# Memory attention moved to the second half of a two-half encoder layer, and the neighbourhood gates moved to the first

## The chip, the cores and the metric

The kernel runs on one core of one Trainium2 chip. The metric is the time of one execution on the device in microseconds, lower is better; quoted is the median of three runs. A profile is one further execution, recorded instruction by instruction. PE is the matrix engine (TensorE), DVE the vector engine, ACT the scalar engine, POOL the GpSimd engine, and SP the queue from which most DMAs are issued.

## What is computed

One layer of an encoder, for two sequences (4096 and 2048 tokens of 1024 numbers) with shared weights. The reference, cut to what matters:

```python
hn = rms_norm(x, norm_g)
proj = hn @ w_in          # na_q na_k na_v na_g | wq wk wv wg | mq mg
ya = neighbourhood_attention(qa, ka, va, rpb) * silu(na_g)   # 6 heads, 8x16 grid window
yb = windowed_gqa(qb, kb, vb, sink) * silu(wg)               # 6 q heads, 2 kv heads, |t-s| <= 128
yc = memory_attention(qc, km, vm) * silu(mg)                 # 4 heads over 256 memory tokens
y = concatenate([ya, yb, yc]) @ w_out
return x + y
```

Queries and keys are RMS-normed per head of 64; the keys and values of the memory come from a small projection of its own. Every product is made with operands split into a high and a low half of float16 (hi and lo): three matmuls (hi hi, hi lo, lo hi) stand for one product in float32.

## The kernel before

The tokens are cut into 24 groups of 256 (16 and 8 for the two sequences), each of two blocks of 128. The kernel has two halves with a change of buffers between them (the seam).

**First half.** For each block, x is loaded, normed, transposed on PE against an identity (line 527) and kept as hi and lo; a copy goes to DRAM (xTd). The projection (`proj`, lines 302, 303, 305) makes a 512-wide chain "a", a 512-wide "b" and a 384-wide "v" of 24 matmuls each. "a" holds the neighbourhood queries and the queries of two of the four memory heads, "b" those of the other two and the neighbourhood keys. The 16 heads are normed (POOL raises to a power, line 311) and transposed on PE, eight transposes per block (line 729). The neighbourhood attention of a group has six units (three head pairs, two kinds of column blocks): scores (line 903), bias and row minimum on DVE (line 920), exponential on ACT (930), hi and lo of the weights (956, 965), one DMA transpose of 12 blocks of 128x128 (`pt<-phl`, line 971), and the product with the values (986). The memory attention of a group has four units of two heads: scores (1042), row minimum (1058), exponential (1064), hi (1078), lo (1084), one DMA transpose of 8 blocks (`ptm<-phm`, line 1092), the product with the memory values (1104). The results of both are stored to DRAM as float32 (`od<-oev`). Beside this the weights of the second half are scaled, split and stored to DRAM.

**Second half.** For each block two 320-wide chains "tok" make the windowed queries, keys and values. For each group eight gate chains of 24 matmuls of 256 columns (lines 1270 to 1272), tanh on ACT (1277) and one DVE step (1282) make `sg`. Windowed attention (1321, 1332 to 1355, DMA transposes of 6 blocks, 1373) follows. The stored results of the other two groups of heads are loaded (`ot<-od`), multiplied by the gates (1413), split to hi and lo (1397, 1403) and go through the output projection (1448 to 1450) with the residual.

The order on every engine is written at build time by a planner (`Plan.run`): tasks with a priority, an assumed duration, buffer counts and dependences are played through, and each engine's instructions are emitted in the order in which the play starts them. On the chip each engine's queue is in order. PSUM has eight banks: two `pj` for projections and gates, four `sc` for scores and transposes, two `po` for attention results. All DMA transposes are issued from SP.

At the seam `f_T2`, `f_TC` and `f_T3` close the pools of the first half and open those of the second; `f_Wa` and `f_Wb` put the second half's weights where the first half's stood, as soon as the last projection has read them. The second group's x (`x2`) lies in a pool that opens at `f_TC`, after the last memory product:

```python
t_x = pl.add("sp", 0.2, f_x, (x_use if gs_ == 0 else [t_TC, t_x]) + [x_st[2 * gs_], x_st[2 * gs_ + 1]], ...)
```

Of the kernel before, what the change touches and what calls it, by code (L numbers as in the profile page):

```python
# [8 lines left out]
F16 = mybir.dt.float16  # L9
# [24 lines left out]
WIN_ORDER = tuple(range(0, 384)) + tuple(range(2560, 2816)) + tuple(range(384, 1152)) + tuple(  # L34
    1536 + 64 * (j + 3 * v) + d for j in range(3) for v in range(2) for d in range(64)) + tuple(range(1920, 2176)) + tuple(
    range(1152, 1536)) + tuple(
# [158 lines left out]
def build(tc, A, out, seqs):  # L195
# [35 lines left out]
    o_d = [[drp.tile([P, 256], F32, name=f"od{g}_{c}", tag=f"od{g}_{c}") for c in range(5)] for g in range(NSB)]  # L231
    mkv_d = [drp.tile([P, 2048], F16, name=f"mkvd{s}", tag=f"mkvd{s}") for s in range(len(seqs))]
    W2 = {"t": 640, "g": D, "o": D}
# [16 lines left out]
    aA, aE = ct("aA", [P, 16]), ct("aE", [P, 16])  # L250
    wA, wE = ct("wA", [P, 8]), ct("wE", [P, 8])
    mA, mE = ct("mA", [P, 4]), ct("mE", [P, 4])
    hg, oc, btmp = ct("hg", [P, 1]), ct("oc", [P, 1]), ct("btmp", [P, 8])
    SC = {}
    for nm in "abvmtgo":
# [8 lines left out]
    for k, n in {"x": 2, "sq": 1, "xhl": 1, "rawm": 2, "sqm": 2, "mkhl": 2, "xT": 2, "raw": 2, "qhl": 1, "khl": 1, "qT": 3, "vhl": 2,  # L264
                 "va": 4, "pf": NPF, "phl": NPHL, "pt": 4, "oev": 3, "pfm": 2, "phm": 2, "ptm": 2, "bE": 2,
                 "ring": 4, "qn": 2, "mkv": 1,
                 "x2": 2, "xr": 2, "qT2": 3, "vw": 8, "pf2": 4,
                 "phl2": 3, "pt2": 2, "tg": 2, "sg": 9, "ot": 4, "yT": 10, "ring2": NR2}.items():
        pl.cap(k, n)
# [116 lines left out]
    wa = pools["WS"].tile([P, 2, NK, 1024], F16, tag="wa", name="wa", bufs=1)  # L386
    wb = pools["WS"].tile([P, 2, NK, 384], F16, tag="wb", name="wb", bufs=1)
    one("SU", "w1f", [P, NK, 1408], F32)
# [3 lines left out]
    W1 = {"a": wa[:, :, :, 0:512], "b": wa[:, :, :, 512:1024], "v": wb, "m": wm}  # L392
# [7 lines left out]
    for s in range(len(seqs)):  # L400
        if s > 0:
            mkv_views(s, one("SM", f"mkvs{s}", [P, 2048], F16))
        for b in range(2):
            one("SM", f"xm{s}{b}", [P, 16, P], F16)
# [36 lines left out]
    for nm, c0, n, src, fl, pr, parts in (("a", 0, 512, w_in, "w1", -29.09, 4), ("b", 512, 512, w_in, "w1", -27.0, 2),  # L441
                                          ("v", 1024, 384, w_in, "w1", -23.0, 2), ("m", 0, 512, A["w_mem_kv"], "wm", -20.0, 2)):
# [3 lines left out]
        for pt_ in range(parts):  # L446
            ks = slice(nk_ * pt_, nk_ * pt_ + nk_)

            def f_l(ks=ks, c0=c0, n=n, src=src, fl=fl):
# [3 lines left out]
                       slack={"v": 12.77, "m": 38.18, "b": 5.95}.get(nm, 0.0))  # L453
# [9 lines left out]
            if nm in 'abvm':  # L463
# [3 lines left out]
        t = scale_tasks(nm, g2, g, ts + [tg2_], pr - 30, parts=parts if nm in 'abvm' else 0)  # L467
# [5 lines left out]
        tb = {"a": ((aA, aE, 0, 6, ph[:, 0:1]), (aA, aE, 6, 2, ph[:, 2:3])), "b": ((aA, aE, 8, 2, ph[:, 2:3]), (aA, aE, 10, 6, iph[:, 0:1])),  # L473
              "m": ((mA, mE, 0, 4, iph[:, 2:3]),)}.get(nm, ())
# [6 lines left out]
    w1_use = [t for nm in "abv" for t in t_w[nm]]  # L481
    su_use = list(t_w["m"])

    def f_TA():
# [4 lines left out]
        mkv_views(0, tile_of("YA", ("mkv", 0), "mkv", [P, 2048], F16))  # L489
    t_TA = pl.add("free", 0.0, f_TA, w1_use, acq=["mkv"], label="TA")  # L490
# [3 lines left out]
    def x_tasks(src, dst_alloc, pr, deps=(), tag=None, acq=()):  # L494
# [25 lines left out]
        for hf in range(2):  # L520
# [9 lines left out]
            t = pl.add("pe", 0.45, f_T, [t, t_id], prio=px - 1.0, acq=[bk] + (list(acq) if hf == 0 else []), rel=["x"] if hf else [], label="xT")  # L530
            if hf:
                x_use.append(t)

# [11 lines left out]

    for i in range(2 * len(seqs)):
# [14 lines left out]
        t_e = pl.add("act", 0.8, f_e, [t_p, t_TA], prio=-3, acq=["rawm"], label="mev")  # L561
# [28 lines left out]
        elif s == 0:  # L590
            t_mk = t_mk0 + [t_kT, t_v]
            su_use += t_mk
        else:
            def f_ms(s=s):
                SY.dma_start(out=mkv_d[s], in_=st[f"mkvs{s}"])
            t_ms = pl.add("sp", 0.1, f_ms, t_mk0 + [t_kT, t_v], prio=-3, label="mst", xf=1.8)
            su_use.append(t_ms)
# [20 lines left out]
    for bt, nm, kw, nr in (("bA", "A", 32, 11), ("bB", "B", 24, 12)):  # L618
        def f_b(bt=bt, nm=nm, n=nr * kw):
            SY.dma_start(out=st[bt], in_=A["rpb" + nm][:, :, 0:n])  # L620
            mk = tile_of("YM", ("mk", nm), "pfm", [P, 2, 256], F32).rearrange("p a k -> p (a k)")[:, 0:n]
            st["mk", nm] = mk
            SY.dma_start(out=mk, in_=A["c_m" + nm])
        t = pl.add("sp", 0.2, f_b, [t_T1], prio=0.9, acq=["pfm"], label="bias", xf=3.0)
# [4 lines left out]
        t_bias.append(pl.add("pool", 4.93, f_b2, [t], prio=0.9, rel=["pfm"], label="bias2"))  # L629
# [5 lines left out]
    kT_done, q_done, qm_done, v_done, xa_use = {}, {}, {}, {}, []  # L635
    x_st = {}
    prev_qk = []
    for gs_ in range(NSB):
        s, g, n = sbs[gs_]
        for blk in range(2):  # L640
# [3 lines left out]
            t_xT = x_tasks(xin[s][row:row + P, :], lambda nb=nb: tile_of("XA", ("xT", nb), "xT", [P, 16, P], F16), pr,  # L644
                           tag=nb, acq=["xT"])
            t_xst = pl.add("pool", 1.04, lambda nb=nb: G.dma_start(out=xT_d[nb], in_=st["xT", nb]), [t_xT], prio=pr + 0.2,
# [3 lines left out]
            def mk_pg(key, n, k0=0, k1=NK, nb=nb):  # L650
                def f():
                    proj(bank("pj", key, nb)[:, 0:n], st["xT", nb], W1[key][:, 0], W1[key][:, 1], slice(0, n), k0, k1)
                return f

            def mk_ev(key, o, n, nb=nb):
                def f():
                    if o == 0:
                        tile_of("X0", ("raw", nb), "raw", [P, 16, HD], F32)
# [7 lines left out]
            for key, nn, o in (("a", 512, 0), ("b", 512, 512)):  # L666
# [12 lines left out]
            pl.add("free", 0.0, lambda: None, [t_p["v"], t_xst], rel=["xT"], label="f")  # L679
            wa_last, wb_last = [t_p["a"], t_p["b"]], [t_p["v"]]  # L680
# [17 lines left out]
            def f_red(nb=nb):  # L698
                st["r16", nb] = small("X0", "r16", 3, 16)
                V.tensor_reduce(out=st["r16", nb], in_=st["sq", nb].rearrange("p (h d) -> p h d", d=HD), axis=AX.X, op=ALU.add)  # L700
            t_red = pl.add("dve", 1.14, f_red, [t_e["b"]], prio=pr - 0.2, rel=["sq"], label="red")
            t_r = pl.add("pool", 3.5, lambda nb=nb: rnorm(st["r16", nb], aA, aE, 16), [t_red] + t_tab,
                         prio=pr - 0.2, label="r16")

            def f_nrm(nb=nb):
                raw = st["raw", nb]
                V.tensor_tensor(out=raw, in0=raw, in1=st["r16", nb].unsqueeze(2).to_broadcast([P, 16, HD]), op=ALU.mult)
            t_nrm = pl.add("dve", 1.14, f_nrm, [t_r], prio=pr - 0.2, label="nrm")

            def f_kg(nb=nb):  # L710
                k = st["raw", nb][:, 10:16]
# [7 lines left out]
            def f_T(i, nb=nb, bks=bks, gs_=gs_, blk=blk):  # L719
                if i == 0:  # L720
                    if blk == 0:
                        tile_of("YA", ("qT", gs_), "qT", [P, 3, 2, 4, 64], F16)
                    tile_of("YA", ("qn", nb), "qn", [P, 2, 2, P], F16)
                raw = st["raw", nb]
                for c in range(4):
                    o = bank(*bks[i])[:, P * c:P * c + P]
                    if i == 0 and c < 3:
                        o = o.rearrange("p (b r c) -> p r b c", r=2, b=4)
                    T.transpose(o, raw[:, 8 * i + 2 * c:8 * i + 2 * c + 2].rearrange("p h d -> p (h d)"), ident)
            t_qk0 = pl.add("pe", 0.5, lambda f_T=f_T: f_T(0), [t_nrm, t_TA, t_id] + prev_qk[0:1], prio=pr - 1.2,  # L730
                          acq=[bks[0], "qn"] + (["qT"] if blk == 0 else []), label="qT")
# [826 lines left out]
```

## Time and profile before

| | |
|---|---|
| median of 3 runs | 2733.17 us (2722.15 to 2733.46) |
| profiled execution | 2732.95 us, of which span 2731.1 us |
| mean granted clock of PE | 0.978 of full speed |
| busy: PE, DVE, ACT, POOL | 2590.1, 1879.7, 1272.5, 543.4 us |
| PE without work, 137 to 1161 us | 82.7 us |
| PE without work, 1161 to 1300 us | 25.4 us |
| PE without work, 1300 to 2732 us | 5.5 us |

The span is the time from the first to the last instruction. A matmul's recorded duration overlaps with the next one's, so the pace of PE is read from start to start and not from durations; idle time of PE is time with no matmul in flight.

### The profile page before, as it was taken

How to read it: one execution, taken by the hardware profiler on the slowest of the kernel's cores; microseconds unless marked ns; L12 is line 12 of the kernel's file. 1: busy time of each engine (PE TensorE's matmuls, PEld its weight loads, DVE VectorE, ACT ScalarE, POOL GpSimd, SP SyncE). 2: the span in 40 equal slices, each digit the busy share in tenths (PEclk: the TensorE clock that was granted, in tenths of full speed). 3: DMA queues.
4: the chain of work that ended last, by engine and by line, in shares of the span. 5: the costliest groups of instructions: out<-in, count | busy, mean ns of one | idle time of the engine just before them, and what ended most of it. 6: DMA issues, size and time to landing. Idle time of an engine off the chain costs nothing.

```text
span 2731.1 us, 58589 instructions
## 1 busy us (share of the span) xinstructions
PE 2590.1 (95%) x22150; PEld 1600.3 (59%) x22150; DVE 1879.7 (69%) x5370; ACT 1272.5 (47%) x3685; POOL 543.4 (20%) x738
## 2 busy tenths in 40 slices
PE   5989888999998899978999999999999999999999
PEld 3545454555554555556666666666666666666665
DVE  6477777888777778885865665666666656566664
ACT  7456555666666667673433333333333333333332
POOL 2553233333322543321000000000000000000000
PEclk9999999999999999988999999999999999999999
DMA  5488997989998998899645444454454435455443
GB/s 182 141 160 175 190 194 186 188 191 201 206 198 181 212 212 168 169 211 261 143 101 105 100 107 106 110 122 112 111 113 104 104 90 106 106 112 122 109 95 76
DMA packets 707467, 401.38 MB, mean 147 GB/s; under 512 B 617648, under 2 KB 654160, under 8 KB 706544
## 3 DMA queue, kind: packets, MB, share of 16 engines
q1 hardware_dynamic: 691312, 347.10, 60.7%
q0 software_dynamic: 15872, 50.55, 5.4%
q8 instruction: 173, 2.83, 0.4%
q14 instruction: 110, 0.90, 0.1%
HBM read 160.54 MB, written 87.03 MB: 91 GB/s over the span
## 4 chain that ended last, share of the span: by engine, by line
PE 56%; DMA 1%; DVE 1%; issue 0%; ACT 0%; POOL 0%; SPq 0%; DVEq 0%; ACTq 0%; POOLq 0%
PE bank L1270 7%; PE bank L1448 6%; PE bank L1271 6%; PE bank L1272 6%; PE bank L1449 6%; PE bank L1450 6%; PE bank L302 4%; PE bank L303 4%; PE bank L305 4%; PE bank L1321 3%; PE bank L1373 3%; DMA pt<-phl 1%; DVE phl L965 0%; PE bank L986 0%; DVE pf L920 0%
## 5 line engine op out<-in xcount | busy, mean ns | idle before, releaser
L1270 PE MATMUL bank<-x,wb 128*128 128x256 f16 x1152 | 315.2, 274 | 0.0
L1271 PE MATMUL bank<-x,wb 128*128 128x256 f16 x1152 | 314.0, 273 | 0.0
L1272 PE MATMUL bank<-x,wa 128*128 128x256 f16 x1152 | 314.0, 273 | 0.0
L1338 ACT ACTIVATE pf<-pf,sm 128x384 f32<-128x384 f32 (+1 forms) x288 | 172.6, 599 | 300.6 <-DVE sm L1332 299.5
L302 PE MATMUL bank<-wa,xT 128*128 128x512 f16 x768 | 299.3, 390 | 4.4 <-DVE vhl L689 3.8
L303 PE MATMUL bank<-wa,xT 128*128 128x512 f16 x768 | 297.9, 388 | 0.7 <-DVE wa L364 0.6
L1448 PE MATMUL bank<-wo,yT 128*128 128x512 f16 x768 | 291.3, 379 | 0.0
L1449 PE MATMUL bank<-wo,yT 128*128 128x512 f16 x768 | 291.1, 379 | 0.0
L1450 PE MATMUL bank<-wo,yT 128*128 128x512 f16 x768 | 291.1, 379 | 0.0
L309 POOL TENSOR_TENSOR r<-r,wA 128x8 f32<-128x8 f32 x48 | 10.3, 215 | 1276.3 <-DVE r L1223 1276.3
L1277 ACT ACTIVATE tg<-bank,hg 128x256 f32<-128x256 f32 x192 | 89.6, 467 | 364.0 <-PE bank L1272 364.0
L311 POOL TENSOR_TENSOR r<-r,mhalf 128x16 f32<-128x16 f32 (+2 forms) x100 | 223.8, 2238 | 7.8
L930 ACT ACTIVATE pf<-pf,sm 128x288 f32<-128x288 f32 (+3 forms) x288 | 156.1, 543 | 128.0 <-DVE sm L920 125.9
L302 PE MATMUL bank<-wa,x 128*128 128x320 f16 x768 | 213.3, 301 | 1.0 <-DMA x<-xTd 1.0
L303 PE MATMUL bank<-wa,x 128*128 128x320 f16 x768 | 213.0, 301 | 0.0
L1463 DVE SCALAR_TENSOR_TENSOR xr<-bank,oc,xr 128x512 f32<-128x512 f32 x96 | 71.9, 749 | 197.8 <-PE bank L1450 197.8
L1332 DVE CUSTOM_DVE_ANT_0 pf<-bank,wtab,nsink 128x384 f32<-128x384 f32 (+1 forms) x288 | 163.9, 599 | 58.6 <-PE bank L1321 58.5
L302 PEld LDWEIGHTS <-xT 128*128 128x128 f16 x1152 | 115.2, 100 | 124.8 <-issue 25.1
L303 PEld LDWEIGHTS <-xT 128*128 128x128 f16 x1152 | 115.1, 100 | 114.5 <-issue 16.3
L305 PE MATMUL bank<-wa,xT 128*128 128x512 f16 x768 | 181.4, 379 | 0.0
L305 PEld LDWEIGHTS <-xT 128*128 128x128 f16 x1152 | 112.8, 98 | 115.7 <-issue 0.3
L1355 DVE SCALAR_TENSOR_TENSOR phl<-pf,sm,phl 128x384 f16<-128x384 f32 (+1 forms) x288 | 174.3, 605 | 8.5
(261 smaller groups left out, 5746.1 us busy)
## 6 DMA issues: line engine op xcount, KB each, us to landing
xTd<-xT POOLq DMA_DIRECT2D x48, 512.0 KB, 4.7
x<-xTd SPq DMA_DIRECT2D x48, 512.0 KB
out<-xr SPq DMA_DIRECT2D x48, 512.0 KB
xx<-in_x_prompt SPq DMA_DIRECT2D x32, 512.0 KB
xr<-in_x_prompt SPq DMA_DIRECT2D x32, 512.0 KB
od<-oev POOLq DMA_DIRECT2D x120, 128.0 KB, 3.8
ot<-od SPq DMA_DIRECT2D x120, 128.0 KB
vd<-vhl POOLq DMA_DIRECT2D x48, 192.0 KB, 4.4
```

The source lines that it names most:

```text
L302: T.matmul(ps, xt[:, kk], wh[:, kk, cols], start=(kk == 0), stop=False)
L303: T.matmul(ps, xt[:, kk], wl[:, kk, cols], start=False, stop=False)
L305: T.matmul(ps, xt[:, NK + kk], wh[:, kk, cols], start=False, stop=(kk == NK - 1))
L311: G.tensor_tensor(out=r, in0=r, in1=mhalf[:, 0:n], op=ALU.pow)
L1270: T.matmul(pv, wh, x[:, :, kk, :], start=(kk == 0), stop=False)
L1271: T.matmul(pv, wh, x[:, :, NK + kk, :], start=False, stop=False)
L1272: T.matmul(pv, wl, x[:, :, kk, :], start=False, stop=(kk == NK - 1))
L1338: S.activation(out=pf[:, 0:nk], in_=pf[:, 0:nk], func=AF.Exp, scale=-1.0, bias=sm[:, 0:1], accum_out=sm[:, 1:2])
L1355: V.scalar_tensor_tensor(out=phl[:, nk:2 * nk], in0=st["pfw", u][:, 0:nk], scalar=st["smw", u][:, 3:4], in1=phl[:, 0:nk], op0=ALU.mult, op ...
L1448: T.matmul(ps, yT[:, 0, ts_], st["wo0"][:, c, cs], start=(ci == 0), stop=False)
L1449: T.matmul(ps, yT[:, 0, ts_], st["wo1"][:, c, cs], start=False, stop=False)
L1450: T.matmul(ps, yT[:, 1, ts_], st["wo0"][:, c, cs], start=False, stop=(ci == 7))
```

## The change

Memory attention (scores, softmax, transposes, product) is taken out of the first half and done per group in the second, where its result goes from PSUM straight into the gate product. Its queries are now made by "tok" (448 wide instead of 320) and transposed by the second half's DMA transpose (10 blocks instead of 6) instead of on PE. The first half's "a" and "b" shrink to 384 columns, and the eight PE transposes of a block become six. The three gate chains of the neighbourhood group are computed in the first half from x of both blocks, so x of a group is kept until then. The neighbourhood result is multiplied by its gate there, split, and stored as hi and lo, so that the second half loads it in the form the output projection reads. The memory's keys and values of both sequences go through DRAM. The first half's weights are now one tile `w1` (4 x 384 columns), freed as a whole; the x of the second group, `x2b`, lies in the same tile. The planner's priority shifts are unchanged.

```diff
-    for nm, c0, n, ... in (("a", 0, 512, ...), ("b", 512, 512, ...), ("v", 1024, 384, ...), ("m", ...)):
+    for nm, c0, n, ... in (("a", 0, 384, ...), ("b", 384, 384, ...), ("v", 768, 384, ...), ("n", 1152, 384, ...), ("m", ...)):
...
-                for c in range(4):
+                for c in range(3):
...
+        for c in range(3):
+            def f_g(gs_=gs_, c=c):
+                x, o = st["xT", gs_], slice(128 * c, 128 * c + 128)
+                pv = bank("pj", "n", gs_, c)[:, 0:256].rearrange("p (b t) -> p b t", b=2)
+                for kk in range(NK):
+                    wh, wl = W1["n"][:, 0, kk, o], W1["n"][:, 1, kk, o]
+                    T.matmul(pv, wh, x[:, :, kk, :], start=(kk == 0), stop=False)
+                    T.matmul(pv, wh, x[:, :, NK + kk, :], start=False, stop=False)
+                    T.matmul(pv, wl, x[:, :, kk, :], start=False, stop=(kk == NK - 1))
...
+                V.scalar_tensor_tensor(out=ov, in0=ov, scalar=GSC, in1=st["sgn", gs_, hp], op0=ALU.mult, op1=ALU.mult)
+                S.activation(out=tile_of("YA", ("yhl", gs_, hp), "yhl", [P, 2, 256], F16)[:, 0], in_=st["oev", gs_, hp], func=AF.Copy)
+                V.tensor_tensor(out=yh[:, 1], in0=st["oev", gs_, hp], in1=yh[:, 0], op=ALU.subtract)
...
-    t_Wa = pl.add("free", 0.0, f_Wa, wa_last + prep_done, label="Wa")
-    t_Wb = pl.add("free", 0.0, f_Wb, wb_last + prep_done, label="Wb")
+        w = pools["WS"].tile([P, 24576], F16, tag="w", name="w2", bufs=1)
+        for k, o, n, m in (("wt0", 0, NK, 896), ("wt1", 7168, NK, 896), ("wgb", 18432, 9, 640)):
+        st["x2b"] = w[:, 14336:18432].rearrange("p (b k t) -> p b k t", b=2, k=16)
+    t_W = pl.add("free", 0.0, f_W, w_last + prep_done, label="W")
...
-        t_x = pl.add("sp", 0.2, f_x, (x_use if gs_ == 0 else [t_TC, t_x]) + ...
+        t_x = pl.add("sp", 0.2, f_x, (x_use if gs_ == 0 else [t_W, t_x]) + ...
...
-                    proj(bank("pj", "t", nb, hf)[:, 0:320], ..., slice(320 * hf, 320 * hf + 320))
+                    proj(bank("pj", "t", nb, hf)[:, 0:448], ..., slice(448 * hf, 448 * hf + 448))
...
-                SY.dma_start_transpose(out=tile_of("XB", ("qT", nb), "qT2", [P, 6, P], F16),
+                SY.dma_start_transpose(out=tile_of("XB", ("qT", nb), "qT2", [P, 10, P], F16),
...
-        for c in range(8):          # gates of the second half
+        for c in range(3, 8):
...
+    for gs_ in range(NSB):          # memory attention, now after the windowed attention's tasks
+        prm = Q0 + gs_ + 0.9
+            t_mk = pl.add("sp", 0.1, f_mk, [t_T2, mkv_st[s]], prio=Q0 + gs_ - 0.6, xf=1.82, acq=["mkv"], label="mk")
...           (units as before; buffers pf2 and phl2 shared with the windowed attention)
+                V.scalar_tensor_tensor(out=sg, in0=bank("po", "m", gs_, hp)[:, 0:256], scalar=GSC, in1=sg, op0=ALU.mult, op1=ALU.mult)
...
-        for ci, c in enumerate((0, 1, 2, 6, 7)):
-            ... load ot, multiply by sg, split to hi and lo
+        for c in range(3):
+            def f_o(gs_=gs_, c=c):
+                SY.dma_start(out=tile_of("YB", ("yT", gs_, c), "yT", [P, 2, 256], F16).rearrange("p a t -> p (a t)"), in_=y_d[gs_][c])
+        for c in (6, 7):
+            y_split(c, [y_mem[gs_, c - 6]])
```

## Rows read from the trace of the kernel before

**Rows 1.** Windows: stretch, length, busy PE, PEld, DVE, ACT, POOL, PEclk, DMA, GB/s.
```profile
0.00:137.00 137.00, 108.70 (x550) 57.29 (x551) 76.23 (x187) 77.88 (x149) 53.34 (x76) 0.96 0.48 161
137.00:1161.00 1024.00, 941.35 (x9680) 541.67 (x9680) 807.25 (x2199) 643.30 (x1782) 370.85 (x489) 0.97 0.90 189
478.00:820.00 342.00, 322.90 (x3554) 189.16 (x3553) 275.73 (x737) 231.09 (x624) 114.53 (x154) 0.99 0.95 197
1024.00:1161.00 137.00, 134.68 (x1514) 77.86 (x1514) 111.70 (x317) 92.06 (x265) 46.46 (x60) 1.00 0.85 168
1161.00:1300.00 139.00, 113.59 (x1394) 82.83 (x1389) 97.38 (x324) 76.76 (x246) 28.36 (x42) 0.84 1.03 232
1300.00:2732.00 1432.00, 1426.49 (x10540) 918.52 (x10538) 898.81 (x2662) 474.52 (x1509) 90.86 (x132) 1.00 0.48 107
```

**Rows 2.** Waits of PE, 137 to 1161 us: total us, times, longest.
```profile
PE bank L986 <- DMA pt<-phl: 37.6, 26, 6.6
PE bank L1104 <- DMA ptm<-phm: 20.4, 9, 4.6
PE bank L903 <- DVE sm L920: 5.4, 2, 4.1
...
PE bank L903 <- ACT pfm L1064: 3.4, 1, 3.4
```

**Rows 3.** Waits of PE, 1161 to 1300 us.
```profile
PE bank L986 <- DMA pt<-phl: 19.0, 13, 3.8
```

**Rows 4.** Timeline of SP's queue in the seam: start us, us, line, DMA.
```profile
1161.04 2.54 SPq L1166 DMA_DIRECT2D wa<-w2dt  x4
...
1243.08 1.07 SPq L1186 DMA_DIRECT2D x<-xTd  x2
```

**Rows 5.** Chain that ended last: start us, us, piece of PE work, instructions.
```profile
1123.52 1.30 PE bank L305 x8
...
1129.97 1.73 PE bank L305 x8
...
1139.42 0.76 PE bank L1042 x12
...
1140.83 1.02 PE bank L729 x8
...
1154.01 0.78 PE bank L1104 x12
...
1259.34 1.09 PE bank L305 x8
```

**Rows 6.** Timeline of PE, first and last of a gate's 24 matmuls.
```profile
1415.13 0.28 PE L1270 MATMUL bank<-x,wb 128*128 128x256 f16 x1
...
1417.65 0.27 PE L1272 MATMUL bank<-x,wgc 128*128 128x256 f16 x1
```

**Rows 7.** DMA queues (packets, MB, share of 16 engines) and transposes issued.
```profile
q1 hardware_dynamic: 691312, 347.10, 60.7%
q0 software_dynamic: 15872, 50.55, 5.4%
...
pt<-phl SPq DMA_TRANSPOSE x432
...
ptm<-phm SPq DMA_TRANSPOSE x96
```

**Rows 8.** DVE's groups of instructions, by shape: count, busy us, mean ns, idle before.
```profile
L1084 DVE SCALAR_TENSOR_TENSOR phm<-pfm,smm,phm 128x256 f16<-128x256 f32 x192 | 87.0, 494 | 0.0
L1282 DVE SCALAR_TENSOR_TENSOR sg<-tg,bank 128x256 f32<-128x256 f32 x192 | 79.5, 414 | 122.4 <-ACT tg L1277 122.4
...
L1058 DVE TENSOR_REDUCE smm<-bank 128x2 f32<-128x512 f32 x96 | 63.7, 682 | 14.2 <-PE bank L1042 14.1
...
L1078 DVE TENSOR_SCALAR phm<-pfm,smm 128x256 f16<-128x256 f32 x192 | 61.3, 361 | 6.3 <-DMA ptm<-phm 3.4 <-DVE smm L1071 0.3
...
L1413 DVE SCALAR_TENSOR_TENSOR sg<-ot,sg 128x256 f32<-128x256 f32 x120 | 50.7, 424 | 3.1
```

More of the change, by code (lines that the diff above doesn't have):

```diff
@@ L480, in build @@
                 t_tab.append(t_t)
[L481 removed]
+    w1_use = [t for nm in "abvn" for t in t_w[nm]]
     su_use = list(t_w["m"])
@@ L643, in build, with xT_alloc @@
             pr = gs_ + 0.5 * blk
-            t_xT = x_tasks(xin[s][row:row + P, :], lambda nb=nb: tile_of("XA", ("xT", nb), "xT", [P, 16, P], F16), pr,
-                           tag=nb, acq=["xT"])
-            t_xst = pl.add("pool", 1.04, lambda nb=nb: G.dma_start(out=xT_d[nb], in_=st["xT", nb]), [t_xT], prio=pr + 0.2,
+            def xT_alloc(gs_=gs_, blk=blk):
+                if blk == 0:
+                    tile_of("XA", ("xT", gs_), "xT", [P, 2, 16, P], F16)
+                return st["xT", gs_][:, blk]
+            t_xT = x_tasks(xin[s][row:row + P, :], xT_alloc, pr, tag=nb, acq=["xT"] if blk == 0 else [],
+                           after=x_first[nb - 1] if blk else None)
+            t_xst = pl.add("pool", 1.04, lambda nb=nb: G.dma_start(out=xT_d[nb], in_=st["xT", nb // 2][:, nb % 2]), [t_xT], prio=pr + 0.2,
                            label="xst", slack=1.595, xf=1.46)
@@ L698, in f_red @@
             def f_red(nb=nb):
[L699 to L702, printed above, removed]
+                st["r16", nb] = small("X0", "r16", 3, 12)
+                V.tensor_reduce(out=st["r16", nb], in_=st["sq", nb][:, 0:768].rearrange("p (h d) -> p h d", d=HD), axis=AX.X, op=ALU.add)
+            t_red = pl.add("dve", 0.87, f_red, [t_e["b"]], prio=pr - 0.2, rel=["sq"], label="red")
+            t_r = pl.add("pool", 3.5, lambda nb=nb: rnorm(st["r16", nb], aA, aE, 12), [t_red] + t_tab,
                          prio=pr - 0.2, label="r16")
@@ new lines, in f_T @@
+                raw = st["raw", nb]
+                for c in range(3):
+                    o = bank(*bks[i])[:, P * c:P * c + P]
+                    if i == 0:
+                        o = o.rearrange("p (b r c) -> p r b c", r=2, b=4)
+                    T.transpose(o, raw[:, 6 * i + 2 * c:6 * i + 2 * c + 2].rearrange("p h d -> p (h d)"), ident)
+            t_qk0 = pl.add("pe", 0.38, lambda f_T=f_T: f_T(0), [t_nrm, t_TA, t_id] + prev_qk[0:1], prio=pr - 1.2,
+                           acq=[bks[0]] + (["qT"] if blk == 0 else []), label="qT")
@@ new lines, in build, with views @@
+            t_qk1 = pl.add("pe", 0.38, lambda f_T=f_T: f_T(1), [t_kg, t_qk0] + prev_qk[1:2], prio=pr - 1.2,
+                           acq=[bks[1]] + (["ring"] if blk == 0 else []), rel=["raw"], label="qT")
+            prev_qk = [t_qk0, t_qk1]
+            def views(i, bks=bks, gs_=gs_, blk=blk):
+                bk = bank(*bks[i])[:, 0:384]
+                if i == 0:
+                    return (bk.rearrange("p (h b t) -> p h b t", h=3, b=4),) + tuple(
+                        st["qT", gs_][:, :, v, :, 32 * blk:32 * blk + 32] for v in range(2))
@@ L1379, in build @@
+    for nb in range(NB):
         pl.add("free", 0.0, lambda: None, win_qk[nb], rel=["qT2"], label="f")
-    for nb in range(NB):
         s = sbs[nb // 2][0]
         users = [k for k in (nb - 1, nb, nb + 1) if 0 <= k < NB and sbs[k // 2][0] == s]
-        pl.add("free", 0.0, lambda: None, [t for k in users for t in win_qk[k]], rel=["ring2"], label="f")
+        pl.add("free", 0.0, lambda: None, [t for k in users for t in win_qk[k][0:3]], rel=["ring2"], label="f")
         pl.add("free", 0.0, lambda: None, [win_pv[k] for k in users], rel=["vw"], label="f")
```

445 lines of the change are left out of this document (217 added, 228 removed).

## Prediction

> **What bounds the kernel now.** I read the windows by stage first [rows 1]. From 1300 us to the end PE is without work for 1432 - 1426.5 = 5.5 us only, at full granted clock: the second half is bound by the matrix engine, with DVE busy 899/1432 = 0.63 and the DMA engines 0.48. From 137 to 1161 us PE idles 1024 - 941.4 = 82.7 us, and its clock is granted at 0.97. Of the two levels, 1.2 and 2.4 GHz, that is 6% of the time at the lower one; with PE busy 0.92 of it some 0.03 x 1024 x 0.92 = 28 us are lost to the clock as well. There DVE is busy 0.79 and DMA 0.90. The seam, 1161 to 1300 us, idles 25.4 us at a clock of 0.84, which costs 0.16 x 139 x 0.82 = 18 us more. The start, to 137 us, idles 28.3 us while weights arrive.
>
> Next I asked for whom PE waits in the first half [rows 2]: 58.0 of the 82.7 us are for DMA transposes, 37.6 for those of the neighbourhood weights (`pt`) and 20.4 for those of the memory weights (`ptm`). The rest are single late DVE or ACT steps, one of them a memory exponential (3.4). In the seam 19.0 us are again for `pt` [rows 3].
>
> So the kernel has a half that lacks nothing but PE time and a half that loses 82.7 + 28 = 111 us of 1024, 10.8%, with PE, DVE and DMA all near their limits. The change moves softmax and transposes out of the tight half and matmuls into it.
>
> **The pace of PE.** From the chain of waits [rows 5], per matmul: 512 columns 1.73/8 = 0.2163 us, 384 columns 1.30/8 = 0.1625, 320 columns 1.09/8 = 0.1363. A gate's matmul of 256 columns takes (1417.65 - 1415.13)/23 = 0.1096 us [rows 6]. The trace has no 448-column chain; it lies between the 384 and the 512, and since the three widths lie on a line I take the middle, 0.1894.
>
> **PE's work, by parts.** (1) First-half projections: 24 x (2 x 0.2163 + 0.1625) = 14.28 us per block become 24 x 3 x 0.1625 = 11.70, so -2.58 x 48 blocks = -123.8. (2) "tok": 48 matmuls per block, each 0.1894 - 0.1363 longer, +2.55 x 48 = +122.4 in the second half (+60 to +184 by the 384 and 512 ends, but (1) and (2) are the same columns and should cancel). (3) Gates: 24 groups x 3 chains x 24 x 0.1096 = 189.4 us go from the second half to the first. (4) Memory scores and products: 48 x 0.76 + 48 x 0.78 = 73.9 us [rows 5] go the other way. (5) Two of a block's eight PE transposes are gone: 1.02/8 x 2 x 48 = -12.2; the second half does them by DMA. First half: -123.8 - 73.9 - 12.2 + 189.4 = -20.5. Second half: +122.4 + 73.9 - 189.4 = +6.9. Together **-13.6 us**. This is the sure part, and small; the rest hangs on idle time.
>
> **What leaves the first half on the other engines.** DVE loses the memory units: 87.0 + 63.7 + 61.3 = 212 us [rows 8], and gains, 72 times, one gate step (0.414), one product (0.424) and one split, priced like the product, so 72 x 1.26 = 91. Its share falls from 0.79 to about (807 - 121)/1024 = 0.67, lower still with 12 heads instead of 16 to norm. SP's queue loses 96 transposes. What those cost the DMA engines: POOL's plain DMAs move 50.55 MB in 5.4% of 2731 us, 343 GB/s [rows 7]. By the code the 528 transposes of rows 7 and the 96 of second-half queries and keys are some 4,576 blocks of 32 KB, 150 MB. At 343 GB/s the other 197 MB of SP's queue take 575 us of its 60.7% x 2731 = 1658; 1083 us are left for the blocks, 0.237 us each, 139 GB/s. The 96 x 8 = 768 memory blocks that go are thus 182 us of DMA time, and the share falls from 0.90 to about 0.72.
>
> The Trainium skill (Advanced Engine Details and Errata, X-Bar Transpose (TRN2)) states that transposing DMAs are as fast as regular ones. By that, an estimate from the plain rate above, the move would relieve the DMA engines by 73 us only; the trace disagrees, with 139 against 343 GB/s. The time that such a small relief gives is the first rival below.
>
> **Idle time of the first half.** The nearest row is 1024 to 1161 us, where the second half's weights are already prepared: DVE 0.82, DMA 0.85, clock 1.00, idle 2.3 of 137 us, 1.7%. The first half after the change has less load than that on both, so I take its rate, 1.7% x 1024 = 17 us, and 6 for the change of sequence, where the edge tables are loaded: 23 instead of 82.7, **-60 us**. The clock fell in the windows that idled and not in this one; I leave 8 of its 28 us: **-20 us**. Bounds: nothing gained, if the waits for `pt` only shift, and all 111.
> The gates make PE fuller, but their input is on chip and they wait for no transpose; each needs a `pj` bank for one ACT and one DVE step after 24 x 0.1096 = 2.6 us of matmuls, and two banks cover that. The neighbourhood result's new steps end in a store that nothing reads before the second half: cost nothing, hidden by the whole seam; without that cover the one visible thing is `f_T3`, which waits for the last store.
>
> **The seam.** Now the x of the second group is issued only at 1243 us [rows 4], since its buffer waits for the last memory product. After the change it lies beside the weights and can come 80 us earlier; tok chains of two groups (2 x 96 x 0.1894 = 36 us) and the first group's five gates (13 us) can fill waits for the last `pt`. No memory unit is left to finish there. Against that, all weights share one tile, so no load starts before the last first-half gate, 8 us after the last projection, and the tok weights are 3.67 MB instead of 2.62. Of 25.4 + 18 = 43 us I take **-20**, bounds +16 (the 3.67 MB at the seam's 232 GB/s, uncovered) and -43.
>
> **The second half's waits.** It gets 212 - 91 = 121 us of DVE work or somewhat more (0.71 instead of 0.63), and 768 + 192 blocks, 227 us of DMA (0.64 instead of 0.48). Lower bound: nothing, as now. Upper: the first half's 10.8%, 155 us. The row nearest in load, 1024 to 1161 us, is busier on both and loses 1.7%, which would be 24 us; I take a third, **+8**. Queued behind a late memory product on PE are tok, gate and output chains for the next group, so each wait is paid in full.
>
> **Start and tail.** At the start the first weights come sooner (384 columns of 512), the fourth set later: 0, between -3 and +10 (1.57 MB at 161 GB/s). At the end the last group's memory units stand in DVE's way: 4 x (0.682 + 2 x 0.361 + 2 x 0.494) = 9.6 us at most; I take **+3**.
>
> **Sum.** The profiled execution took 2732.95 us, the median of the runs 2733.17, so it may stand for them. 2732.95 - 13.6 - 60 - 20 - 20 + 8 + 3 = **2630 us**. Its own range, 2585 to 2680: all idle of the first half gone and the seam clean at the low end, half of the gains at the high end.
>
> **Rivals.**
> - *The transposes that go buy little.* The `pt` waits are the transposes' own latency and the planner's order, not crowding. Then 37.6 us of `pt` waits stay and 6 at the change of sequence, 44 instead of 23; clock loss 14 instead of 8; the seam gives 14 instead of 20: 2630 + 21 + 6 + 6 = 2663. For it: at 478 to 820 us DMA is at 0.95 and PE still idles only 19 of 342. Against it: at 0.85 the waits all but vanish.
> - *The seam gets longer.* PE runs dry between the last gate and the first tok, 16 us and 5 of low clock: 2630 + 20 + 21 = 2671. For it: the single tile. Against: two neighbourhood groups are still to be finished then.
> - *Slower: the second half takes over the first half's trouble.* Place: memory transposes of 8 blocks enter SP's in-order queue among the windowed ones, over three shared `phl2` buffers and four `sc` banks, and PE's in-order queue waits for `ptm` or the windowed `pt` as the first half does now. At 10.8%: 2630 - 8 + 155 = 2777. It decides from (2733 - 2630 + 8)/1432 = 7.8% on. For it: the shifts were not set for this order, and 10.8% was lost at DVE 0.79. Against: DVE 0.71, DMA 0.64, and five gates and four tok chains per group that wait for nothing.
> - *No change:* the same at 7 to 8.7%, about 2733.
>
> **Chances.** Forecast 0.55, little relief 0.13, longer seam 0.09, no change 0.08, slower 0.15. A measurement of this kernel tells about 0.5% (14 us) from nothing. The first three are faster by more: 0.77. Range: from 2575, which takes in the upper bounds of the gains, to 2720, past the two weaker gains; outside are the slower case and a sliver.
>
> **What the next profile would show.** Right: PE idle under 40 us between 137 us and the end of the first half, clock 0.99 there, no wait for `ptm` in it, `pt` waits under 20; the first half shorter by about 100 us, the second longer by 10 to 20; DMA share about 0.7 and 0.64, DVE about 0.67 and 0.71. Wrong if PE shows waits for `ptm` or the windowed `pt` in the second half that add up to more than 30 us, if its clock falls there, or if `pt` waits of the first half stay near 38.

## The result, and the profile after

The changed kernel takes 2686.99 us, the median of four runs (2681.55 to 2698.51), against 2731.03 us (2722.15 to 2733.46) for the kernel before, timed beside it: a ratio of 0.985, 95% interval 0.9807 to 0.9894. It is faster, by 44 us, where 103 were forecast. The profiled execution took 2681.55 us (span 2679.4, mean granted clock 0.990), the quickest of the four; two of the others were at a clock of 0.985. Against the profiled execution before (span 2731.1) 51.7 us are to be explained.

The windows by stage, cut as in [rows 1] (the first half ends when the first tok weights are issued, now at 1133 us):

```profile
0.00:137.00 137.00, 109.81 (x661) 69.95 (x662) 73.68 (x185) 80.33 (x157) 54.62 (x83) 0.96 0.52 176
137.00:1133.00 996.00, 936.82 (x10549) 643.27 (x10547) 672.01 (x1772) 590.14 (x1489) 326.78 (x449) 0.99 0.68 167
478.00:820.00 342.00, 327.21 (x3858) 227.91 (x3857) 225.08 (x608) 212.43 (x533) 110.20 (x150) 1.00 0.65 152
1133.00:1300.00 167.00, 148.81 (x1239) 85.13 (x1239) 118.32 (x364) 77.79 (x244) 29.70 (x35) 0.94 0.81 196
1300.00:2680.00 1380.00, 1373.68 (x9611) 772.36 (x9609) 1015.52 (x2964) 516.42 (x1666) 116.19 (x123) 1.00 0.58 124
```

DVE's share of the first half fell from 0.79 to 672/996 = 0.67 and that of the DMA engines from 0.90 to 0.68, about as forecast. PE's idle time there did not follow: 59.2 us where 82.7 were, and 23 were forecast. From 478 to 820 us the DMA share fell from 0.95 to 0.65, and PE idles 14.8 us instead of 19. The second half is as dense as before (6.3 us idle, clock 1.00) although DVE rose to 0.74 and the DMA engines to 0.58.

Waits of PE from 137 to 1133 us: total us, times, longest (compare [rows 2]):

```profile
PE bank L1013 <- DMA pt<-phl: 38.9, 22, 5.7
PE bank L730 <- DVE sm L947: 4.7, 4, 2.3
PE bank L527 <- DVE xx L517: 4.6, 1, 4.6
```

The waits for `ptm`, 20.4 us, are gone with the memory units. Those for `pt`, 37.6 before, are all still there, which the prediction named as a sign that it is wrong. From 1133 to 1300 us (compare [rows 3]), and the second half:

```profile
PE bank L930 <- DVE sm L947: 5.4, 8, 1.6
PE bank L303 <- DMA w<-w2dt: 3.8, 1, 3.8
PE bank L1013 <- DMA pt<-phl: 3.2, 2, 2.4
...
PE bank L302 <- DMA w<-w2dt: 0.8, 1, 0.8
...
PE bank L1342 <- DVE sm L1273: 1.2, 2, 1.0
```

Here the `pt` waits fell from 19.0 to 3.2 us; 4.6 us are a wait for the tok weights. After 1300 us nothing waits for a transpose; L1342, the memory scores, waits 1.2 us for a bank.

SP's queue in the seam (compare [rows 4]), and two pieces of the chain that ended last, a 384-wide and a 448-wide one (compare [rows 5]):

```profile
1131.97 0.92 SPq L1127 DMA_DIRECT2D w<-xTd  x2
1132.94 2.43 SPq L1108 DMA_DIRECT2D w<-w2dt  x4
```

```profile
1119.48 1.30 PE bank L305 x8
...
1182.65 1.51 PE bank L305 x8
```

The second group's x (`w<-xTd`) is now issued at 1132 us instead of 1243, and the weights at 1132.9, after the last gate. The 384-wide matmul takes 1.30/8 = 0.1625 us, as before, and the 448-wide 1.51/8 = 0.1888; 0.1894 was assumed.

DMA queues, and three of the moved or added DVE groups (compare [rows 7, 8]):

```profile
q1 hardware_dynamic: 710176, 346.57, 57.5%
q0 software_dynamic: 13568, 44.25, 4.5%
```

```profile
L1385 DVE SCALAR_TENSOR_TENSOR phl<-pf,smm,phl 128x256 f16<-128x256 f32 x192 | 83.9, 479 | 0.0
L1378 DVE TENSOR_SCALAR phl<-pf,smm 128x256 f16<-128x256 f32 x192 | 59.1, 350 | 25.9 <-DMA pt<-phl 23.5
L1034 DVE SCALAR_TENSOR_TENSOR oev<-oev,sgn 128x256 f32<-128x256 f32 x72 | 32.9, 456 | 2.5
```

The memory softmax costs DVE nearly the same in its new place (479 and 350 ns, 494 and 361 before), and the gate product 456 ns where 424 were assumed.

**Where the 51.7 us came from.** Idle time of PE: first half 82.7 - 59.2 = 23.5, seam 25.4 - 18.2 = 7.2, start 1.1, second half -1.2: 30.6 us. PE's busy time fell by 2590.1 - 2569.1 = 21.0 us. Summed over windows of 10 us, the busy time lost to the lower clock fell from 42.7 to 18.6 us (first half 24.6 to 8.8, seam 14.5 to 6.0), 24 us. So by this estimate all of the fall in busy time is clock, and PE's work itself grew by about 3 us where 13.6 less were forecast.

### The profile page after: what moved, and what is told of

Same layout as the page of the kernel before. It is cut to its first block, busy times and chain, and to the rows that moved or that the text cites. A ratio compares the mean times of both kernels' runs of the same rounds, so it can differ in the third digit from the quotient of the medians.

```text
span 2679.4 us, 57715 instructions
## 1 busy us (share of the span) xinstructions
PE 2569.1 (96%) x22056; PEld 1570.7 (59%) x22056; DVE 1879.5 (70%) x5283; ACT 1264.7 (47%) x3553; POOL 527.3 (20%) x690
## 4 chain that ended last, share of the span: by engine, by line
PE 55%; DMA 4%; DVE 3%; ACT 1%; POOL 0%; issue 0%; SPq 0%; ACTq 0%; DVEq 0%; POOLq 0%
PE bank L1485 6%; PE bank L302 6%; PE bank L1487 6%; PE bank L1486 6%; PE bank L303 6%; PE bank L305 5%; PE bank L1211 4%; PE bank L1213 4%; PE bank L1212 4%; PE bank L1262 3%; PE bank L1314 2%; DMA pt<-phl 1%; PE bank L1405 1%; PE bank L1342 1%; DMA xx<-in_w_out 1%; DVE phl L1296 1%
## 5 line engine op out<-in xcount | busy, mean ns | idle before, releaser
L302 PE MATMUL bank<-w,xT 128*128 128x384 f16 x1152 | 382.8, 333 | 2.3 <-ACT sq L666 1.3
L303 PE MATMUL bank<-w,xT 128*128 128x384 f16 x1152 | 381.4, 332 | 1.0 <-DVE w L364 0.7
L309 POOL TENSOR_TENSOR r<-r,wA 128x12 f32<-128x12 f32 x48 | 16.3, 340 | 1253.2 <-DVE r L1164 1253.2
L311 POOL TENSOR_TENSOR r<-r,mhalf 128x12 f32<-128x12 f32 (+1 forms) x100 | 224.4, 2244 | 7.8
L305 PE MATMUL bank<-w,xT 128*128 128x384 f16 x1152 | 210.9, 326 | 0.0
L992 DVE SCALAR_TENSOR_TENSOR phl<-pf,sm,phl 128x288 f16<-128x288 f32 (+3 forms) x288 | 148.1, 546 | 44.5 <-ACT phl L983 43.4
L983 ACT ACTIVATE phl<-pf,sm 128x288 f16<-128x288 f32 (+3 forms) x288 | 144.8, 545 | 42.0 <-ACT pf L957 22.4
L1291 DVE TENSOR_SCALAR phl<-pf,sm 128x384 f16<-128x384 f32 (+1 forms) x288 | 119.2, 414 | 57.0 <-DMA pt<-phl 40.2
L770 PE MATMUL bank<-xT,w 128*128 128x256 f16 x576 | 157.6, 274 | 0.0
L771 PE MATMUL bank<-xT,w 128*128 128x256 f16 x576 | 157.0, 273 | 0.0
L772 PE MATMUL bank<-xT,w 128*128 128x256 f16 x576 | 157.0, 273 | 0.0
L1364 ACT ACTIVATE pf<-bank,smm 128x256 f32<-128x256 f32 x192 | 88.9, 471 | 123.9 <-DVE smm L1358 122.4
```

The costliest lines, as they stand in the source:

```text
L302: T.matmul(ps, xt[:, kk], wh[:, kk, cols], start=(kk == 0), stop=False)
L303: T.matmul(ps, xt[:, kk], wl[:, kk, cols], start=False, stop=False)
L305: T.matmul(ps, xt[:, NK + kk], wh[:, kk, cols], start=False, stop=(kk == NK - 1))
L311: G.tensor_tensor(out=r, in0=r, in1=mhalf[:, 0:n], op=ALU.pow)
L770: T.matmul(pv, wh, x[:, :, kk, :], start=(kk == 0), stop=False)
L771: T.matmul(pv, wh, x[:, :, NK + kk, :], start=False, stop=False)
```

## The experiments

Ratios are to the kernel before, timed beside each. "First half" is the stretch from 137 us to the issue of the first tok weights, cut anew in each kernel.

### Memory attention left out of either kernel

The memory units (scores, softmax, transposes, products) are left out; the kernel before loads stored neighbourhood results in place of the memory's, the changed one scales the gate alone.

```diff
-    for gs_ in range(NSB):          # before: memory units of the first half
...
+                SY.dma_start(out=tile_of("YB", ("ot", gs_, c), "ot", [P, 256], F32), in_=o_d[gs_][ci % 3])
```
```diff
-    # after: memory units of the second half
...
+                V.scalar_tensor_tensor(out=sg, in0=sg, scalar=GSC, in1=sg, op0=ALU.mult, op1=ALU.mult)
```

> The kernel before, with the memory attention left out of the first half (no scores, softmax, transposes, product or stores of it; the second half loads neighbourhood results in its place, so its work is unchanged). Load theory (the prediction's: waits of the first half come from the load that the memory units put on DVE, the DMA engines and SP's queue): PE loses 74 to 84 us of work, and idle between 137 us and the end of the projections falls from 82.7 to about 25, pt waits from 37.6 to under 15: about 2580 us. Rival, preparation theory (the pt waits come from the preparation of the second half's weights beside it): only the ptm waits and a few late ACT steps go, pt waits stay above 30: about 2620 us.

> The changed kernel, with the memory attention left out of the second half (the gate product reads the gate alone; queries are still made, normed and transposed). If memory costs the second half only its matmuls (48 x 1.54 us and some 100 breaks between chains of 0.09 us): 80 us less, about 2607. If it also makes PE wait or breaks up the order: more than 95 less, below 2592.

Measured: 2626.59 us (0.9625, 0.9608 to 0.9642) for the kernel before without them, 2599.40 us (0.9541) for the changed one. Windows and `pt` waits of the first half of the kernel before without memory:

```profile
137.00:1083.00 946.00, 881.24 (x8888) 499.05 (x8886) 626.94 (x1632) 558.92 (x1429) 349.56 (x448) 0.97 0.75 176
```
```profile
PE bank L986 <- DMA pt<-phl: 39.9, 23, 5.7
```

With DMA at 0.75 and DVE at 0.66 the `pt` waits are 39.9 us; they were 37.6 at 0.90 and 0.79. So relieving DMA and DVE does not shorten them: the load theory behind the -60 us falls, the time is near the 2620 us of the other expectation, and my rival "the transposes that go buy little" names the right mechanism. The traces say the same of the transposes themselves. From the start of its issue on SP to its last completion mark in the trace, a `pt` transpose of the first half took 5.02 us in the mean in the kernel before (124 transposes), 5.04 without memory (130) and 4.91 in the changed kernel (132), at DMA shares of 0.90, 0.75 and 0.68. Leaving out memory attention gave about 103 us in the kernel before and 87.6 in the changed one.

### The neighbourhood gates left out of either kernel

The three chains, their tanh and their DVE step are left out; the neighbourhood result is multiplied by itself in place of its gate.

```diff
-        for c in range(8):
+        for c in range(3, 8):        # before
...
-        for c in range(3): ...       # after: f_g, f_t, f_sg of the first half
```

> The kernel before, with the three neighbourhood gates left out of the second half (their result is squared instead of gated). The second half is paced by PE, so 72 chains of 2.63 to 2.72 us go: 189 to 196 us less, about 2540. If another engine sets the pace of the second half once these are gone: less is gained, above 2560.

> The changed kernel, with the three neighbourhood gates left out of the first half (the result is squared instead of gated; their weights are still loaded and split). If the gates cost their PE time (72 x 2.68 = 193 us) and cover no waits: about 2494. If they fill waits that come back without them (the reason to have them in the half that waits): PE idle of the first half rises by 30 us or more from 54, and the time is above 2520.

Measured: 2541.06 us (0.9313) and 2610.93 us (0.9565). The gates cost about 188 us in the second half, which is their 189 us of matmuls, and only 76 us in the first. The first half of the changed kernel without them, and its longest waits:

```profile
137.00:1085.00 948.00, 797.73 (x9085) 508.27 (x9084) 661.68 (x1774) 566.92 (x1465) 325.00 (x451) 0.91 0.81 177
```
```profile
PE bank L990 <- DMA pt<-phl: 78.0, 26, 7.8
PE bank L730 <- DVE sm L924: 33.0, 9, 10.4
PE bank L907 <- DVE sm L924: 15.7, 9, 6.4
```

PE idles 150 us there, and the clock falls to 0.91: the gates fill time in which PE would wait. Read crosswise, the four kernels say roughly which half of the change pays; roughly, because the memory queries and the new seam go along in both comparisons. With no memory attention anywhere, moving the gates takes 2626.6 to 2599.4, 27 us less. With no gates anywhere, moving memory takes 2541.1 to 2610.9, 70 us more: of the 210 us of PE work that leave the first half (projections, memory, transposes) it gives up 74 (it ends at 1085 us instead of 1159), and most of the rest turns into waits (150 us of idle time instead of 81) and low clock (0.91 instead of 0.96), while the time from there to the end grows from 1382 to 1525 us. Together the two moves give 44 us, because the gates fill what memory leaves. A kernel in which memory alone moves and all gates stay in the second half was not run.

### The preparation of the second half's weights left out

Loads, maxima, scaling and splits are left out and the scales set to one; the stores to DRAM stay, so that the second half reads the same amount.

```diff
-            t = pl.add("sp", 0.1, f_l, ..., label="wpl", ...)     # load, maximum, scale
-                t = pl.add("act", n / 1200 + 0.2, f_h, ..., label="wph")
-                t = pl.add("dve", n * 1.04e-3 + 0.13, f_lo, ..., label="wplo")
```

> The changed kernel without the preparation of the second half's weights: no loads of w_in and w_out for it, no maxima, no scaling and splitting; only the stores to DRAM stay, of other data, so the second half computes with other weights. Preparation theory: pt waits of the first half fall from 35 us to under 12, its idle from 54 to under 25, clock near 1.00: about 2645 us. Rival, order theory (pt waits come from where the planner's assumed times put the products in PE's in-order queue, whatever runs beside): pt waits stay above 25, about 2680 us.

> The kernel before without the preparation of the second half's weights, as in the run on the changed kernel. Preparation theory: pt and ptm waits together fall from 58 us to under 25 and the time to about 2675. Load theory: with memory still there DMA and DVE stay above 0.75 and the waits above 35, about 2705. Order theory: waits stay near 55, about 2715.

Measured: 2651.82 us (0.9721) for the changed kernel, 35 us under it; 2711.47 us (0.9949) for the kernel before, 18 to 20 us under it. Windows, then waits, of the first half, changed kernel first:

```profile
137.00:1104.00 967.00, 937.91 (x10571) 640.90 (x10570) 630.17 (x1677) 570.75 (x1472) 323.46 (x446) 0.99 0.63 150
```
```profile
PE bank L975 <- DMA pt<-phl: 22.3, 14, 4.9
```
```profile
137.00:1144.00 1007.00, 943.37 (x9844) 542.24 (x9846) 768.42 (x2149) 638.64 (x1791) 367.75 (x492) 0.97 0.84 172
```
```profile
PE bank L948 <- DMA pt<-phl: 44.7, 31, 4.4
PE bank L1066 <- DMA ptm<-phm: 10.5, 3, 6.5
```

In the changed kernel idle time falls from 59.2 to 29.1 us and `pt` waits from 38.9 to 22.3, though DVE goes only from 0.67 to 0.65 and DMA from 0.68 to 0.63. (The expectations cut the first half at about 1096 us, and so start from 54 and 35.) The time is near the preparation theory's, the waits lie between the two. In the kernel before the order theory was right: the waits for `pt` and `ptm` stay at 55.2 us, the `pt` waits alone rise from 37.6 to 44.7, and idle time falls only from 82.7 to 63.6. So the preparation is not what makes PE wait for `pt` in general. What its absence changes in the changed kernel is not shown: the steps are gone from the queues, and the planner also writes another order for everything else.

The longest wait of the changed kernel shows how one comes about (DVE, SP's queue, then PE; start us, us):

```profile
410.09 0.51 DVE L992 SCALAR_TENSOR_TENSOR phl<-pf,sm,phl 128x288 f16<-128x288 f32 x1
...
410.85 0.51 DVE L992 SCALAR_TENSOR_TENSOR phl<-pf,sm,phl 128x288 f16<-128x288 f32 x1
```
```profile
410.57 2.50 SPq L795 DMA_DIRECT2D va<-vd  x4
413.24 6.59 SPq L998 DMA_TRANSPOSE pt<-phl  x1
```
```profile
417.38 1.46 PE L305 MATMUL bank<-w,xT 128*128 128x384 f16 x8
424.52 1.17 PE L1013 MATMUL bank<-pt,va 96*64 96x128 f16 x24 [5.68 <-DMA pt<-phl]
...
425.92 0.53 PE L303 MATMUL bank<-w,xT 128*128 128x384 f16 x1
426.24 0.53 PE L302 MATMUL bank<-w,xT 128*128 128x384 f16 x1
...
429.96 0.33 PE L302 MATMUL bank<-w,xT 128*128 128x384 f16 x1
430.12 0.33 PE L303 MATMUL bank<-w,xT 128*128 128x384 f16 x1
```

The lo steps (L992) of these weights end at 411.4 us; of the preparation only one maximum (1.21 us) stands on DVE between their hi steps and them. SP issues their transpose at 413.2, right behind four loads of the neighbourhood's values (`va`). It holds SP's queue for 6.59 us and lands at 424.5, 11.2 us after its issue, and PE stands for 5.68 us. This is how most of the waits come about: 33.8 of the 38.9 us fall on 15 transposes whose last forerunner in SP's queue is a load of x or of `va`, 4.8 us on six that come behind transfers of the preparation. Among all 132 the landing took 4.4 us in the mean where nothing had been issued on SP in the 3 us ahead (67 transposes), 6.8 right behind a load of x (18) and 10.2 right behind loads of `va` (3). After the wait PE's matmuls start 0.32 us apart instead of 0.16, the lower of the two clocks, for 4 us. Not every wait has that: between 137 and 1133 us the granted clock falls six times in the changed kernel, twelve times between 137 and 1161 us in the kernel before, and the three longest of the 22 `pt` waits each fall together with one of the six.

### The planner told that transposes land later

One assumed duration: how long a neighbourhood transpose occupies the planner's one DMA queue. With the planner's other constants it lands 4.3 us after its issue at the earliest in the play; the edit makes that 5.7. The traces have 4.9 in the mean.

```diff
-label="pT", xf=1.35)
+label="pT", xf=2.25)
```

> The changed kernel with the planner told that a neighbourhood transpose occupies the DMA queue 1.67 times as long; the instructions are the same, only their order changes. Order theory: products stand later in PE's queue, pt waits fall under 12 us and the time to about 2655. Preparation theory: waits turn up elsewhere (buffers held longer, other bursts), idle of the first half stays within 10 us of 54 and the time within 10 us of 2687.

> The kernel before, with the same one number changed that gave the changed kernel 15 us: the planner is told 2.25 us instead of 1.35 for the landing of a neighbourhood transpose. Theory (the waits for pt are a matter of the order written out, in either kernel): they fall from 37.6 to about 15 us between 137 and 1161 us, half of that comes back as other waits, 2731 - 15 = about 2716, and the gain of the change measured against this kernel stays near 45 us. Rival (before the change the DMA engines at 0.90 make the transposes late whatever the order): pt waits stay over 30 us, 2731 or more, and the order helps only after the change has relieved the DMA engines.

Measured: the changed kernel 2672.41 us (0.9795, 0.9780 to 0.9810), 15 us better; the kernel before 2754.08 us (1.0091, 1.0073 to 1.0109), 23 to 26 us worse. First halves and `pt` waits, changed kernel first:

```profile
137.00:1120.00 983.00, 937.14 (x10547) 643.85 (x10546) 681.90 (x1772) 582.48 (x1489) 330.74 (x450) 0.98 0.72 169
```
```profile
PE bank L1013 <- DMA pt<-phl: 13.6, 8, 4.7
PE bank L730 <- POOL raw L715: 6.0, 8, 1.7
PE bank L302 <- ACT sq L666: 5.7, 2, 4.2
```
```profile
137.00:1185.00 1048.00, 958.93 (x9822) 552.30 (x9817) 820.55 (x2226) 652.14 (x1807) 371.27 (x489) 0.95 0.89 186
```
```profile
PE bank L986 <- DMA pt<-phl: 26.7, 10, 7.6
PE bank L1104 <- DMA ptm<-phm: 16.3, 7, 5.1
```

In the changed kernel `pt` waits fall to a third at a higher DMA share, 0.72, and although the transposes take longer to land, 5.31 us in the mean: the waits are the order's. Other steps take their place in part (idle time 59.2 to 45.9 us), so that the time stays above the 2655 us of the order theory. The gain of 15 us is that of the medians; the two intervals just touch. In the kernel before `pt` waits fall by only 11 us, and its idle time rises from 82.7 to 89.1 us with the clock at 0.95; in that order the transposes take 5.82 us to land instead of 5.02. The same edit pays only after the change. Both expectations for the kernel before miss the size; the rival was nearer. Whether another order would be better there is not shown by this one, nor why its transposes land later and its clock falls.

### Both at once

> The changed kernel with both: the planner told the later landing, and the preparation of the second half's weights left out (scales set to one, no loads, maxima and splits; the stores to DRAM stay). Alone the two gave -15 and -35 us against the changed kernel. Theory (two separate causes of the idle time in the first half, the order and the preparation's steps in the queues): they add to about -50 us, 2637, with under 20 us of idle time between 137 us and the end of the first half; that is the level that the prediction took for granted. Rival (both take away the same waits): no further gain, about 2650, idle 28 or more.

Measured: 2638.98 us (0.9670, 0.9655 to 0.9684), 48 us under the changed kernel; the two alone gave 15 and 35.

```profile
137.00:1082.00 945.00, 929.08 (x10550) 639.90 (x10549) 630.17 (x1668) 564.61 (x1464) 325.48 (x446) 0.99 0.65 154
```

PE idles 15.9 us in 945. They add up, and the idle rate is 1.7%, the very rate that the prediction carried over. So it can be had, but by another order and in a kernel that leaves out the preparation, which the layer needs.

### The weights tile in two

The first half's gate weights get a tile of their own, so that the tok weights may be loaded as soon as the last projection has read theirs.

```diff
-    w1 = pools["WS"].tile([P, 4, 2, NK, 384], F16, tag="w", name="w1", bufs=1)
+    w1 = pools["WS"].tile([P, 3, 2, NK, 384], F16, tag="w", name="w1", bufs=1)
+    w1n = pools["WS"].tile([P, 2, NK, 384], F16, tag="wn", name="w1n", bufs=1)
```

> The changed kernel with the one weights tile cut in two: projections' weights and neighbourhood gates' weights. The tok weights and the second group's x go to the first part, whose buffer is free 8 us earlier, at the last projection instead of the last gate. Seam theory: PE waits for the tok weights (4.6 us) and runs at the lower clock around them because their loads start late; tok starts some 8 us earlier, idle of the seam falls from 23 to about 14 us, the time by 8 to 12 us. Rival: the loads wait in SP's queue or for the DMA engines behind transposes, the seam's idle stays within 4 us of 23 and the time within 5 us.

> The changed kernel with the later landing and with the weights tile in two, so that the tok weights load from the last projection on. Alone they gave -15 us and nothing, the second because its seam got 6 us shorter in idle time and its first half 6 us longer. Theory (the seam's gain is real, the loss in the first half was an accident of the order): 2672 - 8 = about 2664. Rival (every change of the order shakes the first half by some 10 us, and nothing adds up): 2665 to 2690.

Measured: 2690.44 us (0.9856, 0.9831 to 0.9880), no gain on the changed kernel; together with the later landing 2668.15 us (0.9778, 0.9762 to 0.9793), 4 us under that edit alone, and the two intervals overlap. With the tile alone the wait of 4.6 us for the tok weights is gone and the seam's idle time falls from 18.2 to 15.6 us, but the first half's rose from 59.2 to 65.2; whether that is the order's accident, as I expected, stays open. The last has the lowest median of the versions that compute the whole layer.

### Gates of the second half back to back

```diff
-            pr = Q0 + gs_ + 0.4 + 0.07 * c
+            pr = Q0 + gs_ + 0.6 + 0.002 * c
```

> The changed kernel with the five gates of a second-half group given nearly one priority, so that they stand back to back in PE's order: 451 instead of 515 changes from one kind of chain to another in the second half. Theory (a change of chain costs PE 0.09 us, which is why the second half's work came out above the sum): 64 x 0.09 = 6 us less PE work there, the period of a group falls from 62.9 to about 62.6 us, if no new waits arise; 2681. Rival (the changes cost nothing): the period stays at 62.9. With either, the gates no longer fill waits between the attention pieces, and idle time in the second half of 10 to 30 us would make it slower than the changed kernel.

Measured: 2700.13 us (0.9903, 0.9876 to 0.9929), 13 us above the changed kernel by the medians, though the two intervals overlap. One gate matmul at the same place of two successive groups, in stretches with no wait, kernel before, changed kernel, and this one:

```profile
1479.01 0.27 PE L1270 MATMUL bank<-x,wb 128*128 128x256 f16 x1
...
1541.21 0.27 PE L1270 MATMUL bank<-x,wb 128*128 128x256 f16 x1
```
```profile
1498.32 0.28 PE L1211 MATMUL bank<-w 128*128 128x256 f16 x1
...
1561.06 0.28 PE L1211 MATMUL bank<-x,w 128*128 128x256 f16 x1
```
```profile
1702.56 0.28 PE L1211 MATMUL bank<-x,w 128*128 128x256 f16 x1
...
1765.08 0.28 PE L1211 MATMUL bank<-w 128*128 128x256 f16 x1
```

The periods are 62.20, 62.74 and 62.52 us. With 64 changes of chain fewer, the work of a group falls by 0.22 us: 24 x 0.22/64 = 0.08 us for a change. That fits the theory of their price. The time went elsewhere: some waits in the second half (3.8 us for `ring`) and, since the planner's order moved everywhere, `pt` waits of 43.6 us in the first half and above all its clock, 0.97.

## Why the prediction was wrong, point by point

- **Idle time of the first half, -60 us: the failed step.** It took the 1.7% of the row 1024 to 1161 us as the rate that a lighter load would give. Measured -23.5 us. The rate was not one of load. From 0.90 to 0.67 of DMA share the `pt` waits stayed at 36 to 45 us under the same assumed duration, in seven kernels with the preparation and all or part of the work (78.0 in the changed one without gates), and the time to land stayed at about 5 us; with another assumed duration the waits fell to 13.6. What sets them is where the products stand in PE's order, and what SP issues just ahead of the transposes. The share itself misled: it adds up the packets' own times, which overlap, and reads 1.03 in the seam [rows 1]. In the reference row the second half's weights were already prepared, which the prediction names. The last of the preparation's splits, kernel before and after:

```profile
991.60 1.28 DVE L822 SCALAR_TENSOR_TENSOR xhl<-xx,sc_ogs,xhl 128x1024 f16<-128x1024 f32 x1
```
```profile
1106.75 1.28 DVE L849 SCALAR_TENSOR_TENSOR xhl<-xx,sc_ogs,xhl 128x1024 f16<-128x1024 f32 x1 [5.18 <-ACT xhl L844]
```

  After the change they run to the end of the first half. But that does not explain the row: without the preparation the kernel before still idles 63.6 of 1007 us, 6.3%. Why the row is so dense stays open. The removal of `ptm` waits (20.4 us) was right, and is nearly the whole gain in idle time.
- **The rival "the transposes that go buy little"** had the mechanism (37.6 us of `pt` waits stay), and its 2663 us is 24 below the median, since it still kept the work term and had no room for the other late steps.
- **PE's work, -13.6 us: mis-sized, about +3.** The pace of the 384 and the 448 columns was right to a thousandth of a microsecond. Missing was the change from one chain to the next: 426 in the second half before, 515 after, 89 x 0.08 = 7 us; with the +6.9 of the sum that is 14, and the period's 24 x 0.54 = 13 agrees. The kernels with parts left out say where it went. With PE's work taken as its busy time less half of that at the lower clock, the gates cost 191 us of work in the second half and 197 in the first, and memory 76 in the first half and 84 in the second; the rest fell by 10 us instead of 13.6. These are rough, since kernels with the same matmuls in another order differ by up to 4 us.
- **Clock of the first half, -20 us:** measured -15.8, granted clock 0.99 as forecast. In part this is luck: the clock was to rise because the idle time goes, and less than half of that went; yet the falls of the clock went from twelve to six.
- **Seam, -20 us:** -7.2 idle and -8.5 clock, -15.7. The early x and the `pt` waits went as forecast; the single tile did cost, 4.6 us of waiting for the tok weights, and a stretch at the lower clock until 1153 us: the rival "longer seam" in small.
- **Second half, +8 and tail +3:** measured about +1 together. The rival that ends slower is refuted: DVE at 0.74 and DMA at 0.58, above the forecast on the first count, and 1.2 us of waits.
- **DMA relief:** the first half's DMA time fell from 0.90 x 1024 to 0.68 x 996, by 244 us, some plain traffic among them. Leaving out memory attention shows it more cleanly: the packets' time on the two queues shown above (before [rows 7] 66.1% of 2731 us, after 62.0% of 2679) fell by 245 us in the kernel before and by 157 in the changed one, of which by the 343 GB/s of plain DMAs some 20 and 3 are not the 768 blocks. So a block took 0.29 us in the one and 0.20 in the other, and the forecast's 0.237 is no constant; the second half's DMA share came out at 0.58, not 0.64. By the rule of the Trainium skill (Advanced Engine Details and Errata, X-Bar Transpose (TRN2)) that the prediction weighed, the relief would have been 73 us, by the prediction's estimate; the trace disagrees, with 154 us or more. The relief was real and bought little time.

## What to carry to other kernels

Where an order is written at build time, a wait for a transfer can be a matter of where the consumer stands in it and of what is issued just ahead of the transfer. Read the time from issue to landing before and after, and change the assumed duration, before you credit a lighter load with the wait; one such edit can also cost time, as it did in the kernel before. Do not carry the idle rate of a dense stretch over to another on the strength of its load alone. Moving work between a stage with gaps and a dense one is worth what fills the gaps: here the moved matmuls that wait for nothing paid, and in the kernels without the neighbourhood gates moving the attention cost 70 us. Count a change from one matmul chain to another as work.

## What the runs showed of the hardware

A change of chain cost PE about 0.08 us beyond the pace of the matmuls (period of a group 62.74 against 62.52 us). After an idle time of 5.68 us PE's matmuls ran 4 us at the lower clock, so that this wait cost some 2 us more than the profile's list of waits says. A DMA transpose of 12 blocks took 4.4 us from issue to landing with nothing issued just ahead of it on its queue, 6.8 behind a load of x and 10.2 behind loads of `va`; its mean was 5.02 us at a DMA share of 0.90 and 4.91 at 0.68.
